# Accumulating the products of a 2x2 block scheme onto each other in PSUM, in a float32 hybrid-attention trunk

## The chip, the cores and the metric

One NeuronCore of a Trainium2 chip runs the whole program. The time is device microseconds of one execution; the median of three runs is given. Lower is better.

## The reference

Two layers of a post-norm trunk over a sequence of 512 positions with 1024 channels, in float32. Each layer projects its input once into ten parts and three gates, runs three mixers on them, and adds a SwiGLU feed-forward part with 2816 hidden channels:

```python
def reference(x, w_in, ...):
    for l in range(DEPTH):                               # DEPTH = 2, x is (1, 512, 1024)
        h = jnp.einsum('bsd,de->bse', x, w_in[l])
        rq, rk, rv, rg, cq, ck, cv, dq, dk, dv, gates = jnp.split(h, splits, axis=-1)
        o_a = _retention(rq, rk, rv, rg, ret_norm_g[l])   # 4 heads, dk 128, dv 256
        o_b = _chunk_attention(cq, ck, cv, ca_rel_bias[l])    # 8 heads of 64
        o_c = _diff_attention(dq, dk, dv, lam, ...)       # 4 heads, two maps each
        g = jax.nn.sigmoid(gates + b_merge[l]).reshape(B, S, N_BRANCHES, D)
        merged = sum over the three branches of g[:, :, i] * (o_i @ w_branch_i[l])
        mix = jnp.einsum('bsd,de->bse', merged, w_out[l])
        x = _layer_norm(DEEPNORM_ALPHA * x + mix, ln1_g[l], ln1_b[l])
        u = jnp.einsum('bsd,df->bsf', x, w_ffn_in[l])
        u_gate, u_up = jnp.split(u, 2, axis=-1)
        ...   # silu(u_gate) * u_up, w_ffn_out[l], second layer norm
```

## The kernel before

Every large operand is kept as a pair of float32r tiles, a high part and the rest, and each product of tiles is three matmuls: high by high, high by low weights, low by high (`mm3`, L122 to L124; which of the three carries which line depends on the side of the weights). A matmul has a 128x128 stationary and a 128x512 moving operand; one PSUM bank holds one 128x512 result, and there are 8 banks.

The wide projections that produce pairs of 512-column blocks (CV with DV, RV with RG, the feed-forward's input, the feed-forward's output) are computed as a 2x2 block problem with seven products instead of eight, in Winograd's form. The products are called m1, m2, y, x, v, g, h. Each has its own sum of activations, made once on VectorE (`Quarters.sums`, L290 ff., for the projections of x; `Twins.sums` for the feed-forward's hidden units), and its own weight block, which is a block of the weights or a sum of blocks (`Close` for the input projection, `Chain` for the feed-forward). Each product makes two 128-row halves, j = 0 and 1, and each half is 4 k-tiles x 3 = 12 matmuls in one PSUM bank where a block has 512 rows of contraction.

Weights go through three stages. SP loads a block of 128x2048 floats into one of four staging buffers; sums of blocks are made by an accumulating DMA that POOL issues (`Halves.more`, L178) or, in `Close`, by VectorE in place (L233, L239). Then ScalarE casts it to the high part (L259) and VectorE subtracts to get the low part (L260); high and low each have a pool of 3 buffers (`wsp`), which a product frees with its last matmul.

`u_two` (L732 ff.) runs one 2x2 problem. Before, m1, y, v and, where it comes ahead of x, g are copied out of PSUM by ScalarE (L746), and VectorE makes the seven sums of the scheme in SBUF for each half: three in `x` (L752 to L754), two in `last_right` (L761, L762), one each in `m2` (L770) and `h` (L775). The results go on to `left_done` and `right_done`, which split them into pairs or apply an activation. The feed-forward's output (`fout_items`) has the same scheme and adds its results to the residual with `plus` (L1302 to L1312), with two copies (L1332, L1339) and three sums (L1345 to L1347) in each half.

The order is a list of items written out by hand: an item is a weight specification and a function, followed by groups of small work (`s_q`, `s_dh`, `s_r1` and so on) which `between()` runs between halves. `run_items` fetches the weights of coming items until three are ready ahead. In each layer's mixer three such problems are named w (CV, DV), p and q (RV with RG, first and second half of the heads). A scheduler then orders the instructions of each engine; an engine runs them in that order, and waits where one is not ready. `w["c"]` and `w["a"]` in the list stand for loading the sums of weight blocks that g and y, h use, ahead of their items.

Of the kernel before, what the change touches and what calls it, by code (L numbers as in the profile page):

```python
# [17 lines left out]
P = 128  # L18
# [38 lines left out]
def trunk(ctx, tc, x_in, xT_in, w_in, ret_norm_g, da_norm_g, lq1, lk1, lq2, lk2, w_a, w_b, w_c, b_merge, w_out,  # L57
# [25 lines left out]
    def bank(name="ps"):  # L83
        return psp.tile([P, 512], F32, tag="ps", name=name)
# [33 lines left out]
        part_hi(pr.hi[:, cols], src, scale)  # L118
        part_lo(pr.lo[:, cols], src, pr.hi[:, cols], scale)

    def mm3(ps, lh, ll, rh, rl, start, stop):
        nc.tensor.matmul(ps, lh, rh, start=start, stop=False)  # L122
        nc.tensor.matmul(ps, lh, rl, start=False, stop=False)  # L123
        nc.tensor.matmul(ps, ll, rh, start=False, stop=stop)  # L124

    class Wt:

# [91 lines left out]
    class Close(Halves):  # L219
# [10 lines left out]
        def v(self):  # L230
            self.d = self.load(1, 1)
            b = self.block(self.d)
            nc.vector.tensor_add(self.d, self.d, self.a)  # L233
            return b

        def m2(self):
# [3 lines left out]
            return b  # L240

        def y(self):
            return self.block(self.__dict__.pop("a"))

        def x(self):
            return self.block(self.__dict__.pop("d"))
# [15 lines left out]
    class Quarters:  # L262
# [26 lines left out]
        def sums(self, t1, t2, scale=None):  # L289
            a, b = self.A, self.B  # L290
            sa, sb = g(name="sa"), g(name="sb")
            nc.vector.tensor_sub(sa[:, a], t1[:, b], t2[:, b])
            nc.vector.tensor_sub(sa[:, b], t1[:, a], sa[:, a])
            nc.vector.tensor_sub(sb[:, a], t2[:, a], sa[:, b])
            nc.vector.tensor_sub(sb[:, b], t1[:, b], t1[:, a])
            p12, p43 = Pair("s12"), Pair("s43")
            split(p12, sa, scale=scale)
            split(p43, sb, scale=scale)
            for name, pr, sl in (("y", p12, a), ("x", p12, b), ("v", p43, a), ("g", p43, b)):
                self.put(name, pr, sl)  # L300

    class Twins:
# [22 lines left out]
        def sums(self, a22):  # L325
            t = g(name="ta")
            nc.vector.tensor_sub(t, self.a21, a22)
            self.part("y", t)
            nc.vector.tensor_sub(t, self.a11, t)
            self.part("x", t)  # L330
            nc.vector.tensor_sub(self.a12, self.a12, t)
            self.part("v", self.a12)
            nc.vector.tensor_sub(self.a21, self.a21, self.a11)
            self.part("g", self.a21)
            self.part("h", a22)

    def product(acts, name, j, wt):

        ps, sl = bank("pf"), slice(P * j, P * j + P)
        for k in range(wt.nk):  # L340
            hi, lo = acts[k].use[name]
            mm3(ps, hi[:, sl], lo[:, sl], wt.hi[:, k], wt.lo[:, k], k == 0, k == wt.nk - 1)
        return ps

    def proj_T(act, wt, c0, nk=KT, ps=None, half=None):
# [261 lines left out]
    def layer(l):  # L607
# [123 lines left out]

        def u_two(hv, acts, left_done, right_done):  # L732

            t = {}

            def it(spec, name, use):
                def fn(wt):
                    for j in range(2):
                        use(j, product(acts, name, j, wt))
                        between()  # L740
                return [spec], fn

            def copy(to):
                def use(j, ps):
                    t[to, j] = g(name="t" + to)
                    nc.scalar.copy(t[to, j], ps)  # L746
                return use

            def x(j, ps):
                u, y, c = g(name="tu"), t["y", j], t.pop(("v", j))  # L750
                t["u", j] = u
                nc.vector.tensor_sub(u, ps, t.pop(("m1", j)))  # L752
                nc.vector.tensor_add(y, y, u)
                nc.vector.tensor_add(c, c, y)  # L754
                right_done(j, c)
                if ("g", j) in t:
                    last_right(j, t.pop(("g", j)))

            def last_right(j, c):
                y, u = t.pop(("y", j)), t["u", j]  # L760
                nc.vector.tensor_add(y, y, c)  # L761
                nc.vector.tensor_add(u, u, c)  # L762
                right_done(2 + j, y)

            def gg(j, ps):
                (last_right if ("u", j) in t else copy("g"))(j, ps)

            def m2(j, ps):
                c = g(name="tm")
                nc.vector.tensor_add(c, t["m1", j], ps)  # L770
                left_done(j, c)

            def h(j, ps):
                u = t.pop(("u", j))
                nc.vector.tensor_sub(u, ps, u)  # L775
                left_done(2 + j, u)

            use = {"x": x, "m2": m2, "g": gg, "h": h}
            return {"c": hv.ahead_c, "a": getattr(hv, "ahead_a", None),
                    **{k: it(getattr(hv, k), k, use.get(k) or copy(k)) for k in ("m1", "g", "v", "m2", "y", "x", "h")}}  # L780

        def rv_done(hp, t, c):
            rv[hp, t] = Pair("rv")
# [337 lines left out]

        w, p, q = u_two(Close(W, 0, 4, (CV, DV)), xq, v_away(cv, 64), v_away(dv, 128)), u_rvg(0), u_rvg(1)
        for (specs, fn), *groups in [
            (u_first(),), (u_gate(0, 1), [s_q(0)], [s_q(1), w["c"]]), (w["m1"], [], [s_q(2), w["a"]]), (u_gate(0, 2), [s_q(3)]),
            (w["g"],), (w["v"],), (w["m2"], [lam]), (w["y"], [p["c"]]), (w["x"],), (u_gate(0, 3),), (w["h"], [p["a"]]),
            (p["m1"], [s_dh(0)]), (p["g"], [], [s_r1(0)]), (p["v"], [s_dh(1)]), (p["m2"], [], [s_r1(1)]),
            (p["y"], [q["c"]]), (p["x"],), (u_rqk(rq, RQ, 1), [q["a"]]), (p["h"],),
            (q["m1"], [], [s_r2(0)]), (u_rqk(rk, RK, 1), [s_r2(1)], [s_r3(0)]), (q["g"], [], [s_r3(1)]),
            (q["v"], [s_dh(2)]), (q["m2"], [], [s_r1(2)]), (q["y"], [s_dh(3)]), (q["x"],), (u_cqk(0), [], [s_r1(3)]), (q["h"],),
            (u_gate(2, 0), [s_r2(2)], [s_r2(3), s_r3(2)]), (u_cqk(1), [s_r3(3)] + c(0)[0], c(0)[1]),  # L1130
            (u_branch(0, 0), c(1)[0] + [v_back(cv)], c(1)[1]), (u_branch(0, 1), *c(2)), (u_cqk(2), *c(3)),
            (u_branch(0, 2), *c(4)), (u_cqk(3), *c(5)), (u_branch(0, 3), *c(6)), (u_gate(2, 1), *c(7)),
            (u_dqk(0), *c(8)), (u_gate(1, 0), [v_back(dv)], [s_c3(7)] + d(0)[1]), (u_branch(1, 0), *d(1)), (u_dqk(1),),
            (u_gate(1, 1), *d(2)), (u_branch(1, 1), *d(3)), (u_dqk(2),),
            (u_gate(1, 2), *d(4)), (u_branch(1, 2), *d(5)), (u_dqk(3),),
            (u_gate(1, 3), *d(6)), (u_branch(1, 3), *d(7)), (u_gate(2, 2), [s_d4(2)], [s_d2(3)]),
            (u_gate(2, 3), [s_d3(3)], [s_d4(3)]),
            (u_branch(2, 0),), (u_branch(2, 1),), (u_branch(2, 2),), (u_branch(2, 3),),
        ]:
            item(specs, fn, *groups)  # L1140
# [175 lines left out]
        def fout_items(gi):  # L1316
# [2 lines left out]
            hv = Chain(w_ffn_out[l], r0, kh)  # L1319
            w = {}  # L1320

            def run(name, j, wt):
                return product([hid[r0 + k] for k in range(kh)], name, j, wt)

            def m1(wt):
                if gi == 0:
                    load_res(saved[2 * l])
                    x2["fresh"] = {(t, hf) for t in range(NT) for hf in range(2)}
                for j in range(2):
                    ps = run("m1", j, wt)  # L1330
                    w[j] = g(name="w")
                    nc.scalar.copy(w[j], ps)  # L1332
                    plus(j, 0, ps, ALU.add)

            def y(wt):
                for j in range(2):
                    ps = run("y", j, wt)
                    w["y", j] = g(name="wy")
                    nc.scalar.copy(w["y", j], ps)  # L1339

            def x(wt):
                for j in range(2):
                    ps = run("x", j, wt)
                    u = w.pop(j)
                    nc.vector.tensor_sub(u, ps, u)  # L1345
                    plus(2 + j, 0, u, ALU.subtract)
                    nc.vector.tensor_add(u, u, w.pop(("y", j)))  # L1347
                    plus(2 + j, 1, u, ALU.add)
                    plus(j, 1, u, ALU.add)

            def one(name, i, hf, op):
                def fn(wt):
                    for j in range(2):
                        plus(2 * i + j, hf, run(name, j, wt), op)
                return fn

            def gg(wt):
                for j in range(2):
                    ps = run("g", j, wt)
                    plus(2 + j, 1, ps, ALU.add)  # L1360
                    plus(2 + j, 0, ps, ALU.subtract)

            return {"c": hv.ahead_c, "m1": ([hv.m1], m1), "y": ([hv.y], y), "x": ([hv.x], x),
                    "m2": ([hv.m2], one("m2", 0, 0, ALU.add)), "v": ([hv.v], one("v", 0, 1, ALU.add)),
                    "g": ([hv.g], gg), "h": ([hv.h], one("h", 1, 0, ALU.add))}

        def fout_rest(hf):

# [108 lines left out]
```

## Time and profile before

| | |
|---|---|
| Median of 3 runs | 1894.03 us (1893.98 to 1894.27) |
| Span of the profiled execution | 1894.5 us, 0.5 us above that median |
| TensorE busy | 1881.4 us, 9170 matmuls |
| VectorE busy | 1355.1 us, 2159 instructions |
| ScalarE busy | 946.2 us, 1575 instructions |
| DMA | 285.11 MB, mean 150 GB/s |

Engines in the rows: PE is TensorE's matmuls, PEld its weight loads, DVE is VectorE, ACT ScalarE, POOL GpSimd, SP SyncE. A row of the groups view names the line, the engine, the operation, the tiles written and read, their count, the busy time in us, the mean ns of one, and behind the second bar the engine's idle time ahead of them with what ended it. A row of the timeline begins with the start and the duration in us; brackets hold the idle time before. A matmul's row lasts longer than the step to the next one, since matmuls overlap. Times are of one profiled execution.

### The profile page before, as it was taken

To read this page: it belongs to the slowest core of one execution; us is meant where nothing else is said; L and a number is where in the kernel's file an instruction comes from. 1 tells how busy PE (TensorE), PEld (TensorE's weight loads), DVE (VectorE), ACT (ScalarE), POOL (GpSimd) and SP (SyncE) were. 2 spreads that over 40 slices of the span, in tenths; PEclk is the share of its full clock that TensorE was granted. 3 is DMA by queue.
4 is the path that set the end of the run, shared out by engine and by line. 5 is a ranking of instruction groups with operands and counts; after the bars stand their busy time and mean duration, and the time that the engine had idled before them with its cause. 6 is when DMAs were issued, how large, how long until landed. Compare 5 with 4: busy or idle time off the path is not lost. (4 is left out here: it accounts for less than half of the span.)

```text
span 1894.5 us, 24166 instructions
## 1 busy us (share of the span) xinstructions
PE 1881.4 (99%) x9170; PEld 1584.9 (84%) x9170; DVE 1355.1 (72%) x2159; ACT 946.2 (50%) x1575; POOL 113.9 (6%) x141
## 2 busy tenths in 40 slices
PE   9999999999999999999999999999999999999998
PEld 7888888888888888888898888888888898888886
DVE  6788867577765866786687788666776668667866
ACT  5555555566634444543255546555765344344430
POOL 2000000000000000000010000000000000000000
PEclk9999999999999999999999999999999999999999
DMA  9585443332155686765475944533322637777561
GB/s 282 170 268 152 122 159 108 122 122 68 57 186 147 156 178 169 207 156 127 139 190 171 285 113 145 169 104 95 123 79 73 205 101 175 181 179 196 139 153 45
DMA packets 239348, 285.11 MB, mean 150 GB/s; under 512 B 8580, under 2 KB 147936, under 8 KB 239232
## 3 DMA queue, kind: packets, MB, share of 16 engines
q1 hardware_dynamic: 215232, 237.01, 38.1%
q0 software_dynamic: 24000, 46.56, 14.4%
q8 instruction: 72, 1.18, 0.3%
q14 instruction: 44, 0.36, 0.1%
HBM read 260.42 MB, written 23.12 MB: 150 GB/s over the span
## 5 line engine op out<-in xcount | busy, mean ns | idle before, releaser
L122 PE MATMUL pt<-xTh,wh 128*128 128x512 f32 (+1 forms) x1328 | 497.2, 375 | 2.3 <-ACT wh L154 2.0
L124 PE MATMUL pt<-xTh,wl 128*128 128x512 f32 (+1 forms) x1328 | 494.0, 372 | 0.0
L123 PE MATMUL pt<-xTl,wh 128*128 128x512 f32 (+1 forms) x1328 | 493.9, 372 | 0.0
L154 ACT CAST wh<-st 128x1024 fp32r<-128x1024 f32 (+1 forms) x236 | 220.2, 962 | 210.4 <-PE pt L123 91.1
L155 DVE TENSOR_TENSOR wl<-st,wh 128x1024 fp32r<-128x1024 f32 (+1 forms) x236 | 257.4, 1111 | 81.0 <-ACT wh L154 75.0
L260 DVE TENSOR_TENSOR wl<-st,wh 128x2048 fp32r<-128x2048 f32 x98 | 224.4, 2290 | 117.2 <-ACT wh L259 116.8
L122 PEld LDWEIGHTS pt<-xTh,wh 128*128 128x128 f32 x1328 | 250.1, 189 | 44.3 <-ACT wh L154 2.5
L124 PEld LDWEIGHTS pt<-xTh,wl 128*128 128x128 f32 x1328 | 250.5, 189 | 43.9
L123 PEld LDWEIGHTS pt<-xTl,wh 128*128 128x128 f32 x1328 | 250.9, 189 | 41.9
L259 ACT CAST wh<-st 128x2048 fp32r<-128x2048 f32 x98 | 187.5, 1913 | 157.4 <-PE pf L124 73.9
L124 PE MATMUL pf<-wh,xTl 128*128 128x512 f32 x240 | 93.4, 389 | 0.0
L123 PE MATMUL pf<-wl,xTh 128*128 128x512 f32 x240 | 93.4, 389 | 0.0
L122 PE MATMUL pf<-wh,xTh 128*128 128x512 f32 x240 | 93.4, 389 | 0.0
L122 PE MATMUL pf<-wh,s43h 128*128 128x512 f32 x192 | 75.5, 393 | 0.1
L122 PE MATMUL pf<-wh,s12h 128*128 128x512 f32 x192 | 74.9, 390 | 0.0
L123 PE MATMUL pf<-wl,s43h 128*128 128x512 f32 x192 | 74.8, 389 | 0.0
L124 PE MATMUL pf<-wh,s12l 128*128 128x512 f32 x192 | 74.7, 389 | 0.0
L123 PE MATMUL pf<-wl,s12h 128*128 128x512 f32 x192 | 74.7, 389 | 0.0
L124 PE MATMUL pf<-wh,s43l 128*128 128x512 f32 x192 | 74.2, 390 | 0.0
L382 ACT COPY sw<-pt 32x512 f32<-32x512 f32 (+1 forms) x96 | 55.7, 580 | 29.2 <-PE pt L124 28.0
L1207 DVE TENSOR_TENSOR fth<-fth,pt 128x512 f32<-128x512 f32 x28 | 19.2, 687 | 56.5 <-PE pt L124 56.2
L124 PEld LDWEIGHTS pf<-wh,xTl 128*128 128x128 f32 x240 | 45.1, 188 | 9.4
(362 smaller groups left out, 3570.7 us busy)
## 6 DMA issues: line engine op xcount, KB each, us to landing
st<-in_w_in SPq DMA_DIRECT2D x60, 1024.0 KB, 5.4
st<-in_w_ffn_in SPq DMA_DIRECT2D x56, 512.0 KB, 5.6
st<-in_w_ffn_out SPq DMA_DIRECT2D x20, 1024.0 KB, 5.0
st<-in_w_in SPq DMA_DIRECT2D x32, 512.0 KB, 5.0
st<-in_w_ffn_in SPq DMA_DIRECT2D x16, 1024.0 KB, 5.8
st<-in_w_ffn_in POOLq DMA_DIRECT2D x16, 1024.0 KB, 9.1
st<-in_w_ffn_out POOLq DMA_DIRECT2D x16, 1024.0 KB, 8.6
st<-in_w_in POOLq DMA_DIRECT2D x12, 1024.0 KB, 11.8
```

The lines of the kernel that those rows point to most:

```text
L122: nc.tensor.matmul(ps, lh, rh, start=start, stop=False)
L123: nc.tensor.matmul(ps, lh, rl, start=False, stop=False)
L124: nc.tensor.matmul(ps, ll, rh, start=False, stop=stop)
L154: return [nc.scalar.copy(self.hi[:, a:b], self.st[:, a:b]), nc.vector.tensor_sub(self.lo[:, a:b], self.st[:, a:b], f(self.hi[:, a:b]))]
L155: nc.vector.tensor_sub(self.lo[:, a:b], self.st[:, a:b], f(self.hi[:, a:b]))]
L259: nc.scalar.copy(self.hi, st)
L260: nc.vector.tensor_sub(self.lo, st, f(self.hi))
L382: nc.scalar.copy(sw[half * b:half * b + half], ps[half * o:half * o + half])
L1207: nc.vector.tensor_mul(t, t, pu)
```

## The change

Seven products are summed in the scheme in chains: m1 is part of x, g and h's results, y part of v's. After the change a product that builds on another writes into its PSUM bank without clearing it first, so the bank holds the running sum: x, g and h add onto m1's bank in this order, and v onto y's. Engines read the bank between the products. For this the activation sums of x, g and v take other signs (in `Quarters.sums` and in `Twins.sums`), so that additions in PSUM give what subtractions gave. In `u_two` three copies per half remain (m1, y, v, each into a result tile), and each of m2, x and g is one VectorE sum onto it; h is read straight from PSUM. In `fout_items` the seven products of a half go to the residual by seven `plus` calls; copies and sums in between are gone. In `Close`, the block "a" is used by y ahead of v. The order of products in the mixer is m1, y, v, m2, x, g, h instead of m1, g, v, m2, y, x, h, and the loads of "a" and "c" change places accordingly; the feed-forward's output keeps its order. `skip_group_check` is a flag for the program's builder.

```diff
-    def mm3(ps, lh, ll, rh, rl, start, stop):
+    def mm3(ps, lh, ll, rh, rl, start, stop, onto=False):
...
-        nc.tensor.matmul(ps, lh, rh, start=start, stop=False)
+        nc.tensor.matmul(ps, lh, rh, start=start, stop=False, skip_group_check=onto)
...
         def v(self):
             self.d = self.load(1, 1)
             b = self.block(self.d)
-            nc.vector.tensor_add(self.d, self.d, self.a)
+            nc.vector.tensor_add(self.d, self.d, self.__dict__.pop("a"))
             return b
...
         def y(self):
-            return self.block(self.__dict__.pop("a"))
+            return self.block(self.a)
...
             nc.vector.tensor_sub(sa[:, a], t1[:, b], t2[:, b])
-            nc.vector.tensor_sub(sa[:, b], t1[:, a], sa[:, a])
-            nc.vector.tensor_sub(sb[:, a], t2[:, a], sa[:, b])
-            nc.vector.tensor_sub(sb[:, b], t1[:, b], t1[:, a])
+            nc.vector.tensor_sub(sa[:, b], sa[:, a], t1[:, a])
+            nc.vector.tensor_add(sb[:, a], t2[:, a], sa[:, b])
+            nc.vector.tensor_sub(sb[:, b], t1[:, a], t1[:, b])
...
-    def product(acts, name, j, wt):
-        ps, sl = bank("pf"), slice(P * j, P * j + P)
+    def product(acts, name, j, wt, ps=None):
+        onto, sl = ps is not None, slice(P * j, P * j + P)
+        ps = ps if onto else bank("pf")
         for k in range(wt.nk):
             hi, lo = acts[k].use[name]
-            mm3(ps, hi[:, sl], lo[:, sl], wt.hi[:, k], wt.lo[:, k], k == 0, k == wt.nk - 1)
+            mm3(ps, hi[:, sl], lo[:, sl], wt.hi[:, k], wt.lo[:, k], k == 0 and not onto, k == wt.nk - 1, onto)
...
-            t = {}
+            t, onto = {}, {"x": "m1", "g": "m1", "h": "m1", "v": "y"}
-            def it(spec, name, use):
+            def it(name, use):
                 def fn(wt):
                     for j in range(2):
-                        use(j, product(acts, name, j, wt))
+                        t[name, j] = ps = product(acts, name, j, wt, t.pop((onto.get(name), j), None))
+                        if name in ("x", "g"):
+                            t["m1", j] = ps
+                        use(j, ps)
                         between()
...
+            def m2(j, ps):
+                c = t.pop(("c11", j))
+                nc.vector.tensor_add(c, c, ps)
+                left_done(j, c)
             def x(j, ps):
...
+                c = t.pop(("c12", j))
+                nc.vector.tensor_sub(c, c, ps)
                 right_done(j, c)
...
             def gg(j, ps):
-                (last_right if ("u", j) in t else copy("g"))(j, ps)
+                c = t.pop(("c22", j))
+                nc.vector.tensor_sub(c, c, ps)
+                right_done(2 + j, c)
...
             def h(j, ps):
-                u = t.pop(("u", j))
-                nc.vector.tensor_sub(u, ps, u)
-                left_done(2 + j, u)
+                left_done(2 + j, ps)
...
-            (q["m1"], [], [s_r2(0)]), (u_rqk(rk, RK, 1), [s_r2(1)], [s_r3(0)]), (q["g"], [], [s_r3(1)]),
-            (q["v"], [s_dh(2)]), (q["m2"], [], [s_r1(2)]), (q["y"], [s_dh(3)]), (q["x"],), (u_cqk(0), [], [s_r1(3)]), (q["h"],),
+            (q["m1"], [], [s_r2(0)]), (u_rqk(rk, RK, 1), [s_r2(1)], [s_r3(0)]), (q["y"], [], [s_r3(1)]),
+            (q["v"], [s_dh(2)]), (q["m2"], [], [s_r1(2)]), (q["x"], [s_dh(3)]), (u_cqk(0), [], [s_r1(3)]), (q["g"],), (q["h"],),
...
+            return {"c": hv.ahead_c, "m1": it("m1", (0, 0, add)), "y": it("y", (1, 1, add)), "x": it("x", (0, 1, sub)),
+                    "m2": it("m2", (0, 0, add)), "v": it("v", (0, 1, add)), "g": it("g", (1, 1, sub)), "h": it("h", (1, 0, add))}
```

More of the change, by code (lines that the diff above doesn't have):

```diff
@@ L119, in split @@
         part_lo(pr.lo[:, cols], src, pr.hi[:, cols], scale)
-    def mm3(ps, lh, ll, rh, rl, start, stop):
-        nc.tensor.matmul(ps, lh, rh, start=start, stop=False)
-        nc.tensor.matmul(ps, lh, rl, start=False, stop=False)
-        nc.tensor.matmul(ps, ll, rh, start=False, stop=stop)
+    def mm3(ps, lh, ll, rh, rl, start, stop, onto=False):
+        nc.tensor.matmul(ps, lh, rh, start=start, stop=False, skip_group_check=onto)
+        nc.tensor.matmul(ps, lh, rl, start=False, stop=False, skip_group_check=onto)
+        nc.tensor.matmul(ps, ll, rh, start=False, stop=stop, skip_group_check=onto)
     class Wt:
@@ L328, in sums @@
             self.part("y", t)
-            nc.vector.tensor_sub(t, self.a11, t)
+            nc.vector.tensor_sub(t, t, self.a11)
             self.part("x", t)
-            nc.vector.tensor_sub(self.a12, self.a12, t)
+            nc.vector.tensor_add(self.a12, self.a12, t)
             self.part("v", self.a12)
-            nc.vector.tensor_sub(self.a21, self.a21, self.a11)
+            nc.vector.tensor_sub(self.a21, self.a11, self.a21)
             self.part("g", self.a21)
             self.part("h", a22)
-    def product(acts, name, j, wt):
-        ps, sl = bank("pf"), slice(P * j, P * j + P)
+    def product(acts, name, j, wt, ps=None):
+        onto, sl = ps is not None, slice(P * j, P * j + P)
+        ps = ps if onto else bank("pf")
         for k in range(wt.nk):
             hi, lo = acts[k].use[name]
-            mm3(ps, hi[:, sl], lo[:, sl], wt.hi[:, k], wt.lo[:, k], k == 0, k == wt.nk - 1)
+            mm3(ps, hi[:, sl], lo[:, sl], wt.hi[:, k], wt.lo[:, k], k == 0 and not onto, k == wt.nk - 1, onto)
         return ps
@@ L732, in u_two @@
         def u_two(hv, acts, left_done, right_done):
-            t = {}
-            def it(spec, name, use):
+            t, onto = {}, {"x": "m1", "g": "m1", "h": "m1", "v": "y"}
+            def it(name, use):
                 def fn(wt):
                     for j in range(2):
-                        use(j, product(acts, name, j, wt))
+                        t[name, j] = ps = product(acts, name, j, wt, t.pop((onto.get(name), j), None))
+                        if name in ("x", "g"):
+                            t["m1", j] = ps
+                        use(j, ps)
                         between()
-                return [spec], fn
+                return [getattr(hv, name)], fn
             def copy(to):
@@ L747, in copy @@
                 return use
+            def m2(j, ps):
+                c = t.pop(("c11", j))
+                nc.vector.tensor_add(c, c, ps)
+                left_done(j, c)
             def x(j, ps):
[L750 to L754, printed above, removed]
-                right_done(j, c)
[L756 to L763, printed above, removed]
-            def gg(j, ps):
-                (last_right if ("u", j) in t else copy("g"))(j, ps)
[L768 to L771, printed above, removed]
-            def h(j, ps):
-                u = t.pop(("u", j))
-                nc.vector.tensor_sub(u, ps, u)
-                left_done(2 + j, u)
-            use = {"x": x, "m2": m2, "g": gg, "h": h}
-            return {"c": hv.ahead_c, "a": getattr(hv, "ahead_a", None),
-                    **{k: it(getattr(hv, k), k, use.get(k) or copy(k)) for k in ("m1", "g", "v", "m2", "y", "x", "h")}}
+                c = t.pop(("c12", j))
+                nc.vector.tensor_sub(c, c, ps)
+                right_done(j, c)
+            def gg(j, ps):
+                c = t.pop(("c22", j))
+                nc.vector.tensor_sub(c, c, ps)
+                right_done(2 + j, c)
+            def h(j, ps):
+                left_done(2 + j, ps)
+            use = {"m1": copy("c11"), "m2": m2, "y": copy("c22"), "v": copy("c12"), "x": x, "g": gg, "h": h}
+            return {"c": hv.ahead_c, "a": getattr(hv, "ahead_a", None), **{k: it(k, fn) for k, fn in use.items()}}
         def rv_done(hp, t, c):
@@ L1123, in layer @@
         for (specs, fn), *groups in [
[L1124 to L1127, printed above, removed]
-            (q["m1"], [], [s_r2(0)]), (u_rqk(rk, RK, 1), [s_r2(1)], [s_r3(0)]), (q["g"], [], [s_r3(1)]),
-            (q["v"], [s_dh(2)]), (q["m2"], [], [s_r1(2)]), (q["y"], [s_dh(3)]), (q["x"],), (u_cqk(0), [], [s_r1(3)]), (q["h"],),
+            (u_first(),), (u_gate(0, 1), [s_q(0)], [s_q(1), w["a"]]), (w["m1"], [], [s_q(2)]), (u_gate(0, 2), [s_q(3), w["c"]]),
+            (w["y"],), (w["v"],), (w["m2"], [lam]), (w["x"], [p["a"]]), (u_gate(0, 3),), (w["g"],), (w["h"], [p["c"]]),
+            (p["m1"], [s_dh(0)]), (p["y"], [], [s_r1(0)]), (p["v"], [s_dh(1)]), (p["m2"], [], [s_r1(1)]),
+            (p["x"], [q["a"]]), (u_rqk(rq, RQ, 1),), (p["g"], [q["c"]]), (p["h"],),
+            (q["m1"], [], [s_r2(0)]), (u_rqk(rk, RK, 1), [s_r2(1)], [s_r3(0)]), (q["y"], [], [s_r3(1)]),
+            (q["v"], [s_dh(2)]), (q["m2"], [], [s_r1(2)]), (q["x"], [s_dh(3)]), (u_cqk(0), [], [s_r1(3)]), (q["g"],), (q["h"],),
             (u_gate(2, 0), [s_r2(2)], [s_r2(3), s_r3(2)]), (u_cqk(1), [s_r3(3)] + c(0)[0], c(0)[1]),
@@ L1320, in fout_items @@
             w = {}
[L1322 to L1349, printed above, removed]
@@ L1351, in one, with it @@
-            def one(name, i, hf, op):
+            def it(name, *adds):
                 def fn(wt):
+                    if name == "m1" and gi == 0:
+                        load_res(saved[2 * l])
+                        x2["fresh"] = {(t, hf) for t in range(NT) for hf in range(2)}
+                    on = {"x": "m1", "g": "m1", "h": "m1", "v": "y"}.get(name, name)
                     for j in range(2):
-                        plus(2 * i + j, hf, run(name, j, wt), op)
-                return fn
@@ L1357, in gg @@
[L1357 to L1365, printed above, removed]
+                        w[on, j] = product([hid[r0 + k] for k in range(kh)], name, j, wt, w.pop((on, j), None))
@@ new lines, in fn @@
+                        for i, hf, op in adds:
+                            plus(2 * i + j, hf, w[on, j], op)
+                        if name in ("m2", "v", "h"):
+                            w.pop((on, j))
+                return [getattr(hv, name)], fn
+            add, sub = ALU.add, ALU.subtract
+            return {"c": hv.ahead_c, "m1": it("m1", (0, 0, add)), "y": it("y", (1, 1, add)), "x": it("x", (0, 1, sub)),
+                    "m2": it("m2", (0, 0, add)), "v": it("v", (0, 1, add)), "g": it("g", (1, 1, sub)), "h": it("h", (1, 0, add))}
```

## The prediction

> **What bounds the kernel now.** The first page of the profile gives the span and the share of each engine.
>
> ```profile
> span 1894.5 us, 24166 instructions
> PE 1881.4 (99%) x9170; PEld 1584.9 (84%) x9170; DVE 1355.1 (72%) x2159; ACT 946.2 (50%) x1575; POOL 113.9 (6%) x141
> ```
>
> TensorE (PE) has work in 1881.4 of 1894.5 us, so 13.1 us are all that could be won without fewer or faster matmuls. Read second: the view of waits, for TensorE alone, in full, and the last row of TensorE in the timeline.
>
> ```profile
> PE pt L122 <- ACT wh L154: 2.0, 1, 2.0
> PE warm L578 <- POOL ident masks.py:199: 1.5, 1, 1.5
> PE px L504 <- DVE z L495: 0.6, 2, 0.3
> PE pt L122 <- ACT xTh L596: 0.2, 1, 0.2
> ```
>
> ```profile
> 1885.44 0.39 PE L124 MATMUL pf<-wh,hidl 128*128 128x512 f32 x1
> ```
>
> The last matmul ends at 1885.83; the 8.67 us behind it are the last layer norm and the store. The waits on L154, on the identity and on L596 (3.7 us together) stand at the start, before the first projection has its weights. Neither stretch is touched by the change: the last product is h before and after, with one vector operation behind it. 13.1 - 8.67 - 3.7 leaves 0.7 us in the whole body, about the 0.6 of L504. So no relief of VectorE (DVE), ScalarE (ACT) or the DMA queues can bring more than 0.7 us. Everything else that the change can do is to make TensorE wait where it doesn't now.
>
> Third, the windows view of a stretch of the FFN, where the 2x2 products are the main work.
>
> ```profile
> 700.00:800.00 100.00, 100.00 (x452) 82.19 (x451) 70.14 (x77) 48.08 (x58) 7.72 (x6) 1.00 0.71 174
> ```
>
> Columns: TensorE, its weight loads, VectorE, ScalarE and POOL busy, granted clock, DMA share, GB/s. TensorE is busy in all 100 us at full clock, VectorE in 70.
>
> **The sums that go.** The groups view prices them (first and last kinds of each, us in total, mean ns of one).
>
> ```profile
> L752 DVE TENSOR_TENSOR tu<-pf,tm 128x512 f32<-128x512 f32 x20 | 13.7, 683 | 0.0
> L761 DVE TENSOR_TENSOR ty<-ty,tg 128x512 f32<-128x512 f32 x12 | 8.2, 684 | 0.0
> L1347 DVE TENSOR_TENSOR w<-w,wy 128x512 f32<-128x512 f32 x8 | 5.3, 685 | 0.0
> L746 ACT COPY tg<-pf 128x512 f32<-128x512 f32 x12 | 6.6, 591 | 10.7 <-PE pf L124 10.7
> L1332 ACT COPY w<-pf 128x512 f32<-128x512 f32 x8 | 4.2, 581 | 0.0
> ```
>
> Two layers with three input groups (w, p, q) and FFN-in's chains make 20 halves of u_two, as x20 shows; FFN-out has 8. In u_two 7 sums become 3: 80 fewer. In FFN-out 3 sums and 8 accumulations into the residual become 7 accumulations: 32 fewer. 112 x 0.684 = 76.6 us of VectorE. Of copies the 12 of g and 16 in FFN-out go: 28 x 0.59 = 16.5 us of ScalarE. By the first part they are worth between 0 and 0.7 us; I take 0, because the waits that they could shorten (L504) are in the layer norm, not among the products. The matmuls stay at 9170, the DMA instructions at their number. The negated sums of activations (Quarters, Twins) replace instructions one for one: nothing.
>
> **The waits that come.** x, g and h now write m1's bank, and v writes y's. Each product must wait until the read of the one below it is over. Where other products stand between, 12 to 24 matmuls and more cover a 0.6-us read. The shortest cover is g to h: h's first half follows g's second half, 12 matmuls after g's first half has ended. Matmuls of this shape follow each other at 0.227 us (in the rows below, 22 steps from 190.35 to 195.34), so the cover is 2.72 us for a subtraction of 0.68. It fails only with a long instruction ahead of it in VectorE's queue: a rival, below. Taken: 0.
>
> **The order that moves.** The groups w, p and q now run m1, y, v, m2, x, g, h instead of m1, g, v, m2, y, x, h. Weight loads move with it: the sums behind "a" are loaded one or more items earlier, those behind "c" later; loads and their accumulations are still issued by SP and POOL at a fetch that runs three weight blocks ahead, 3 x 24 x 0.227 = 16 us, and the page has them land sooner (its last figure, from issue to landing):
>
> ```profile
> st<-in_w_in SPq DMA_DIRECT2D x60, 1024.0 KB, 5.4
> ...
> st<-in_w_in POOLq DMA_DIRECT2D x12, 1024.0 KB, 11.8
> ```
>
> So I take 0; an accumulation issued one product late would still have 5 us. One spot costs. In the compiled order of the changed kernel, after the second rk projection of group q, TensorE has: 8 transposes (L861, now L853), the 24 matmuls of y, 8 transposes, and then x's first two matmuls, which need its high weights, then its third, with the low weights; only seven x matmuls later come m2 and v. Before, the same place held 8 transposes, 24 matmuls of g, 8 transposes and v, whose weights had long been cast. The weight pool has 3 buffers; y, v and m2 hold them. x is the fourth, so its cast (L259) can't start until y's last matmul has ended, and its subtraction (L260) follows the cast. The instructions on ScalarE and VectorE stand there in the same order before and after; only the weights that are cast differ. So the trace of before shows when they can be ready. Timelines of TensorE, ScalarE and VectorE:
>
> ```profile
> 189.01 0.39 PE L124 MATMUL pt<-xTh,wl 128*128 128x512 f32 x1
> 189.24 0.93 PE L861 MATMUL prt<-ident,ro 128*128 128x128 f32 x7
> ...
> 190.35 0.40 PE L123 MATMUL pf<-wl,s43h 128*128 128x512 f32 x1
> ...
> 195.34 0.39 PE L124 MATMUL pf<-wh,s43l 128*128 128x512 f32 x1
> 195.58 1.03 PE L861 MATMUL prt<-ident,ro 128*128 128x128 f32 x8
> 196.37 0.48 PE L122 MATMUL pf<-wh,s43h 128*128 128x512 f32 x1
> 196.68 0.40 PE L123 MATMUL pf<-wl,s43h 128*128 128x512 f32 x1
> 196.91 0.39 PE L124 MATMUL pf<-wh,s43l 128*128 128x512 f32 x1
> ```
>
> ```profile
> 195.78 1.91 ACT L259 CAST wh<-st 128x2048 fp32r<-128x2048 f32 x1 [3.46 <-PE pf L124]
> 199.26 1.07 ACT L746 COPY tg<-pf 128x512 f32<-128x512 f32 x2
> ```
>
> ```profile
> 194.56 2.29 DVE L239 TENSOR_TENSOR st<-st 128x2048 f32<-128x2048 f32 x1
> 196.76 0.68 DVE L386 TENSOR_TENSOR rot<-rot,sw 128x512 f32<-128x512 f32 x1
> 197.71 2.29 DVE L260 TENSOR_TENSOR wl<-st,wh 128x2048 fp32r<-128x2048 f32 x1 [0.27 <-ACT wh L259]
> 199.92 0.68 DVE L112 TENSOR_TENSOR rqkl<-rot,rqkh 128x512 fp32r<-128x512 f32 x1
> 200.53 2.06 DVE L114 SCALAR_TENSOR_TENSOR oal<-prt,colv,oah 128x512 fp32r<-128x512 f32 x3
> ```
>
> The 24th matmul issues at 195.34 and ends at 195.73; the cast starts at 195.78 and ends at 197.69; the subtraction starts at 197.71 and ends at 200.00. TensorE wants x's first matmul at 196.37, so it waits 1.32 us. It issues two, and wants the third at 196.91 + 1.32 = 198.23, but the low weights are there at 200.00: 1.77 more. Together 200.00 - 196.91 = 3.1 us, and some hundredths to hand on. Behind it seven matmuls of x end their issue at 201.6: m2's bank must have been read by the first of the three L114, which ends at 200.53 + 0.69 = 201.2, and v's bank by the two copies, here tg, that end at 200.3. Both are in time, by 0.4 and more, so nothing is added. The second layer has the same spot:
>
> ```profile
> 1138.02 0.39 PE L124 MATMUL pf<-wh,s43l 128*128 128x512 f32 x1
> ```
>
> ```profile
> 1138.82 2.29 DVE L260 TENSOR_TENSOR wl<-st,wh 128x2048 fp32r<-128x2048 f32 x1 [0.27 <-ACT wh L259]
> ```
>
> 1138.82 + 2.29 - 1138.02 = 3.1. TensorE has nothing else queued that it could take, since its instructions run in order, and no slack later, so both stalls reach the end: 2 x 3.1 and the handing on, +6.3 us. Other spots of the new order (v after y in the first group, FFN-in's second chain) I estimate by the same kind of sum at +-0.3 each, with both signs, net 0, and give them +-1.5 in the range. The profiled span is 1894.5, the median of the runs 1894.0; the difference of 6.3 is put on the median: **1900.3 us**.
>
> **Rivals.** *The clock falls with the stall.* At the start of the trace one wait of 2.03 us is followed by slow matmuls (timeline of TensorE; then the windows view, whose third value from the right is the granted clock):
>
> ```profile
> 7.77 0.80 PE L122 MATMUL pt<-xTh,wh 128*128 128x512 f32 x1 [2.03 <-ACT wh L154]
> 8.36 0.63 PE L123 MATMUL pt<-xTl,wh 128*128 128x512 f32 x1
> 8.79 0.63 PE L124 MATMUL pt<-xTh,wl 128*128 128x512 f32 x1
> ```
>
> ```profile
> 9.00:10.00 1.00, 1.00 (x3) 0.78 (x3) 1.00 (x3) 0.84 (x2) 0.54 (x1) 0.50 1.11 302
> 11.00:12.00 1.00, 1.00 (x6) 0.82 (x5) 0.74 (x2) 0.01 (x1) 0.00 (x0) 0.98 1.17 269
> ```
>
> Steps of 0.43 us for about 3.3 us, 8 matmuls at 0.20 extra: 1.6 us for each stall, 3.2 for both, 1903.5. For it: the wait here is of that size, 1.3 and 1.8 with two matmuls between. Against: those two matmuls break it, and the start had other idle time ahead of it. Chance 0.17. The Trainium skill, "TensorE: Matmul & The Clock Gate", section "Part 1: The HAM clock gate", says that half clock returns only after a whole idle window of about 3.4 us, counted in windows that run free of the kernel; by that rule neither wait is enough and the time stays at the forecast. The trace does not bear it out cleanly: a wait of 2.03 us stood before the half clock.
>
> *Every h waits for its g.* If a 2.29-us subtraction starts just ahead of g's read, the read ends 2.97 us after g, plus 0.16 by which a matmul's 0.39 outlasts its 0.23 step, against a cover of 2.72: 0.4 late. In 28 places at most 11.5 us, 1911.8. It decides once VectorE is more than 1.9 us behind as g's half ends. For it: fetches put a cast and a subtraction at about every product. Against: the VectorE queue loses sums exactly there, and a subtraction starts at the end of a product two or three items back, not at g's half. Chance 0.09; a part of it, some 3 us, is likelier than all. The Trainium skill, "PSUM — Partial Sum Buffer", section "The four PSUM rules", allows a synchronised read in the middle of an accumulation, so that the read is a wait and not an error; no row of before shows such a read.
>
> *Not slower: x's weights are ready.* It decides if x's subtraction ends 3.1 us earlier, by 196.91, or its cast finds a buffer that y doesn't hold, or if only one layer has the spot (+3.1). Then the time is 1894 less at most 0.7: 1893.3 to 1897.2. For it: in the trace of before no weight of a 2x2 product was waited for. Against: the cast in the trace starts 0.05 after the matmul that frees the buffer, with no wait left to take out. Chance 0.09. Faster by over 0.2% would need more than the 0.7 us that exist, so a fault in my reading of the page: 0.03.
>
> **How the numbers follow.** Forecast 0.62, clock 0.17, h 0.09, not slower 0.09, faster 0.03. 0.2% is 3.8 us, about what a measurement of this kernel can tell from no change. The range: at the low end 1896.0, between both cases; at the high end 1905.0, which takes in the clock with 1.5 of unknown. It leaves out the full price of h and the time under 1896. Slower is 0.62 + 0.17 + 0.09 = 0.88, same 0.09, faster 0.03.
>
> **What the profile after would show.** Right: TensorE's waits list L122 and L123 (x's products, in pf) behind ACT wh L259 with about 1.3 and DVE wl L260 with about 1.8, twice each, near 196.4 and 1137.5; TENSOR_TENSOR 112 fewer on VectorE, about 1279 us busy; TensorE's matmuls still 9170 and the end of its last one about 6 us later. Clock rival: a granted clock under 1.00 right behind these places. h rival: waits of pf on DVE lines of the subtractions in gg and plus, 28 times. Wrong: none of these waits, or a TensorE wait in a third place that is larger.

## The result and the profile after

The changed kernel takes 1904.7 us (median of 4 runs, 1903.87 to 1905.45) against 1894.15 before: ratio 1.0053, 95% interval 1.0038 to 1.0067. A second measurement gave 1903.59 against 1894.12, ratio 1.0046 (1.0034 to 1.0059). So it is 9.5 to 10.5 us slower; 6.3 were forecast. Executions of every kernel here, the one before too, fall into two groups some 1.8 us apart, by the traces according to whether the slow matmuls at the start last until 5 to 7 us or until about 11, so a median of four can lie between the groups; both profiles compared here are of the longer one.

The first page of the profile after, its span and engines:

```profile
span 1903.7 us, 24003 instructions
PE 1886.1 (99%) x9170; PEld 1588.1 (83%) x9170; DVE 1290.6 (68%) x2047; ACT 931.2 (49%) x1547; POOL 114.0 (6%) x141
```

VectorE has 112 instructions and 64.5 us less, ScalarE 28 and 15.0 less, and the span is 9.2 us longer. (A run's time is about 1.8 us above its span, here 1905.45 and 1903.7, so the span of before, 1894.5, is to be set beside spans and not beside the median.) The view of waits of the changed kernel, TensorE alone, in full:

```profile
PE pf L123 <- DVE wl L260: 3.2, 2, 1.6
PE pf L122 <- ACT wh L259: 2.2, 2, 1.1
PE warm L579 <- POOL ident masks.py:199: 1.5, 1, 1.5
PE pt L122 <- ACT wh L154: 0.8, 1, 0.8
PE px L505 <- DVE z L496: 0.6, 2, 0.3
PE pf L122 <- ACT rph L106: 0.4, 2, 0.2
```

The first two rows are new: x's products wait for the low weights twice and for the high weights twice, 5.4 us as this view counts idle time (it counts from the end of a matmul's row, which outlasts the step to the next one). The last row is new too. The timelines of TensorE, ScalarE and VectorE at the first of the two places, in the first layer:

```profile
195.37 0.39 PE L124 MATMUL pf<-wh,s12l 128*128 128x512 f32 x1
195.60 1.03 PE L853 MATMUL prt<-ident,ro 128*128 128x128 f32 x8
197.75 0.73 PE L122 MATMUL pf<-wh,s12h 128*128 128x512 f32 x2 [1.11 <-ACT wh L259]
200.08 0.50 PE L123 MATMUL pf<-wl,s12h 128*128 128x512 f32 x1 [1.59 <-DVE wl L260]
200.42 0.39 PE L124 MATMUL pf<-wh,s12l 128*128 128x512 f32 x1
...
203.39 0.39 PE L124 MATMUL pf<-wh,s43l 128*128 128x512 f32 x1
```

```profile
195.80 1.90 ACT L259 CAST wh<-st 128x2048 fp32r<-128x2048 f32 x1 [3.46 <-PE pf L124]
```

```profile
197.73 2.29 DVE L260 TENSOR_TENSOR wl<-st,wh 128x2048 fp32r<-128x2048 f32 x1 [0.26 <-ACT wh L259]
```

y's last matmul issues at 195.37; the cast into its buffer runs from 195.80 to 197.70, the subtraction from 197.73 to 200.02. x's first two matmuls issue at 197.75, the third at 200.08. Without the wait the first would stand at 196.39 and the third at 196.93: 3.15 us. The second layer has the same places, and something more:

```profile
1142.29 0.73 PE L122 MATMUL pf<-wh,s12h 128*128 128x512 f32 x2 [1.12 <-ACT wh L259]
1144.62 0.80 PE L123 MATMUL pf<-wl,s12h 128*128 128x512 f32 x1 [1.59 <-DVE wl L260]
1145.21 0.63 PE L124 MATMUL pf<-wh,s12l 128*128 128x512 f32 x1
...
1150.74 0.40 PE L124 MATMUL pf<-wh,s43l 128*128 128x512 f32 x1
```

```profile
1143.00:1144.00 1.00, 0.03 (x1) 0.00 (x0) 1.00 (x1) 1.00 (x3) 0.00 (x0) 0.94 0.00 0
...
1146.00:1150.00 4.00, 4.00 (x11) 3.06 (x10) 1.80 (x3) 0.05 (x1) 0.00 (x0) 0.50 0.96 326
```

The matmuls behind the stall take 0.63 instead of 0.39 and follow at 0.43 instead of 0.227, and the windows view gives the granted clock, third from the right, as 0.50. The 0.94 of the window ahead means that the clock fell at 1143.88, inside the second idle piece and not behind it. The last slow step ends at 1150.74. The fourteen steps from 1144.62 to there take 6.12 us; the same fourteen in the first layer, from 200.08 to 203.39, take 3.31. That is 2.8 us more. So in this execution: two stalls 6.3, half clock behind one of them 2.8, two waits of h (below) 0.8. That is 9.9; the last matmul of the kernel issues 9.14 us later than before (1885.44 to 1894.58). The rest is 0.5 less in the first 15 us and small differences in other places, of both signs.

```profile
1894.58 0.39 PE L124 MATMUL pf<-wh,hidl 128*128 128x512 f32 x1
```

### The profile page after: what moved, and what is told of

It reads as the page before. It is cut to its first block, busy times and chain, and to the rows that moved or that the text cites. A ratio compares the mean times of both kernels' runs of the same rounds, so it can differ in the third digit from the quotient of the medians.

```text
span 1903.7 us, 24003 instructions
## 1 busy us (share of the span) xinstructions
PE 1886.1 (99%) x9170; PEld 1588.1 (83%) x9170; DVE 1290.6 (68%) x2047; ACT 931.2 (49%) x1547; POOL 114.0 (6%) x141
## 5 line engine op out<-in xcount | busy, mean ns | idle before, releaser
L750 ACT COPY tc<-pf 128x512 f32<-128x512 f32 x60 | 34.1, 586 | 54.2 <-PE pf L124 53.0
```

## The experiments

Theory S: x in group q is taken ahead of its weights, 3.1 us in each layer, and the stall lets the clock fall, for the rest. Rival A: the accumulation is dear in itself. Rival B: the new order of products is, whatever is accumulated.

**The same kernel again** (no edit).

> The changed kernel once more, unedited, for a second trace. Theory S (the two stalls for x's weights in group q cost 2 x 3.1 us, and half clock behind them the rest): both stalls at the same places and of the same length, 1.3 and 1.8 us each; matmuls at a step of 0.43 us behind one or both of them, in blocks of about 3.3 us, and the time between 1903.8 and 1905.5 according to how many blocks there are, 1.6 us for each. Rival A (the accumulation itself is dear, by waits for reads spread over the 28 places): no relation between the time and the slow blocks.

It took 1903.59 us (1902.44 to 1904.60 in 5 runs), 0.2 under the range that was expected. In its trace the two rows of the waits for x's weights are those of the first trace, figure for figure. The timeline of TensorE and two windows:

```profile
197.72 0.52 PE L123 MATMUL pf<-wl,s12h 128*128 128x512 f32 x1 [1.59 <-DVE wl L260]
...
198.47 0.63 PE L122 MATMUL pf<-wh,s12h 128*128 128x512 f32 x1
```

```profile
198.00:199.00 1.00, 1.00 (x4) 0.76 (x4) 1.00 (x3) 1.00 (x2) 0.00 (x0) 0.53 0.14 10
...
1143.00:1144.00 1.00, 0.18 (x1) 0.19 (x2) 1.00 (x2) 1.00 (x4) 0.00 (x0) 0.77 0.00 0
```

The stalls are the same. The slow steps now stand behind both: eight in the first layer, 1.6 us, and seven in the second, 1.45 us, where the first trace had none behind the first stall and fourteen behind the second, 2.8 us. By the windows, the clock fell at 198.06 and at 1143.55 (0.53 and 0.77 are mixtures of 1.00 and 0.50), each time for 3.41 us. So the part of the clock varies in place between executions and was about the same in sum in these two, 3.0 and 2.8; that it explains each run's time can't be shown from two traces.

**Something between y and v.** Two items of the list change places in q:

```diff
-            (q["m1"], [], [s_r2(0)]), (u_rqk(rk, RK, 1), [s_r2(1)], [s_r3(0)]), (q["y"], [], [s_r3(1)]),
+            (q["m1"], [], [s_r2(0)]), (q["y"], [s_r2(1)], [s_r3(0)]), (u_rqk(rk, RK, 1), [], [s_r3(1)]),
```

> In group q the second rk projection comes behind y instead of ahead of it, so its 24 matmuls lie between y and v, x's weights have time, and nothing waits for the cast that needs y's buffer; accumulation, sums and all else as in the changed kernel. Theory S: both stalls and the slow blocks behind them go, 10 to 11 us less than the changed kernel, 1893.5 to 1894.8, as before. Rival A: the accumulation is unchanged, so 1903 or more.

1893.90 us; ratio to before 0.9998 (0.9989 to 1.0007). The view of waits of TensorE in full:

```profile
PE warm L579 <- POOL ident masks.py:199: 1.5, 1, 1.5
PE pt L122 <- ACT wh L154: 0.7, 1, 0.7
PE px L505 <- DVE z L496: 0.6, 2, 0.3
PE pf L122 <- ACT rph L106: 0.4, 2, 0.2
PE pt L122 <- ACT xTh L597: 0.3, 1, 0.3
```

Neither wait for x's weights is there, no slow matmul stands in the body, and the time is that of before. All the accumulation is still in, so Rival A falls: the whole loss that can be told hangs on that one place of the order.

**The order alone.** The kernel before with the list of items of the changed one and, in Close, y ahead of v:

```diff
-            (q["m1"], [], [s_r2(0)]), (u_rqk(rk, RK, 1), [s_r2(1)], [s_r3(0)]), (q["g"], [], [s_r3(1)]),
-            (q["v"], [s_dh(2)]), (q["m2"], [], [s_r1(2)]), (q["y"], [s_dh(3)]), (q["x"],), (u_cqk(0), [], [s_r1(3)]), (q["h"],),
+            (q["m1"], [], [s_r2(0)]), (u_rqk(rk, RK, 1), [s_r2(1)], [s_r3(0)]), (q["y"], [], [s_r3(1)]),
+            (q["v"], [s_dh(2)]), (q["m2"], [], [s_r1(2)]), (q["x"], [s_dh(3)]), (u_cqk(0), [], [s_r1(3)]), (q["g"],), (q["h"],),
...
-            nc.vector.tensor_add(self.d, self.d, self.a)
+            nc.vector.tensor_add(self.d, self.d, self.__dict__.pop("a"))
...
-            return self.block(self.__dict__.pop("a"))
+            return self.block(self.a)
```

> The kernel before with the new order of products alone (m1, y, v, m2, x, g, h, with the loads of a and c moved), sums and copies as before, each product in a bank of its own. Theory S: x needs a free bank like the others, so it isn't taken ahead of v, whose weights are there; no stall, 1893.5 to 1895.0. Rival B (the order alone makes the stall, by the moved weight loads and sums): two stalls of about 3 us, 1900 or more.

1893.64 us, ratio 0.9996 (0.9987 to 1.0005). Waits of TensorE, in full:

```profile
PE warm L578 <- POOL ident masks.py:199: 1.5, 1, 1.5
PE pt L122 <- ACT wh L154: 0.6, 1, 0.6
PE px L504 <- DVE z L495: 0.6, 2, 0.3
```

No stall, so Rival B falls too. (The copies are not quite as before: with g behind x its 12 copies go, 1563 ScalarE instructions against 1575.) It takes both: in the new order v follows y, and with the accumulation v waits until ScalarE has read y's bank, while x, which adds onto a bank long read, waits for no bank. That this is why the scheduler puts x there is read from the compiled orders of the two kernels; it was not tried by itself.

**Work in the stall.** Ahead of x in q, zeros are added onto m1's bank, and x is queued behind them:

```diff
+    def fill(ps, acts):
+        with tc.issue_after(end_mm["y"].ins):
+            for i in range(14):
+                end_mm["fill"] = nc.tensor.matmul(ps[0:64], zero, acts[0].wide, start=False, stop=False, skip_group_check=True)
```

> The changed kernel with 14 matmuls of a zero stationary operand (128x64, moving 128x512) added onto m1's bank ahead of x in group q, so 3.2 us of work that adds zero stands in each stall. Theory S, with the clock as the second part: the weights are late as before, so the 6.3 us stay, but TensorE is never idle for long, so the slow steps go: 1900.3 to 1901.5, 3 to 4 us under the changed kernel. If the clock is not the second part, the time stays at 1904 to 1905.

1900.96 us: 2.6 to 3.7 under the two medians of the changed kernel, inside the expected range. Waits of TensorE, in full:

```profile
PE warm L589 <- POOL ident masks.py:199: 1.5, 1, 1.5
PE px L515 <- DVE z L506: 0.6, 2, 0.3
PE pf L123 <- ACT rph L107: 0.4, 2, 0.2
PE pt L123 <- ACT wh L155: 0.3, 1, 0.3
```

TensorE does 28 useless matmuls (6.4 us) in place of two stalls, and no step of 0.43 us stands in the body. The zeros end just ahead of the weights: in the first layer the subtraction for the low weights ends at 197.94, and the first matmul that needs them issues at 198.00. So this is the price of late weights by itself, 6.8 us over before (6.3 at the stalls and h's wait, told last), and the rest of the loss is the clock's.

**Half the fill.** As above with `range(7)`.

> As fill, with 7 zero matmuls instead of 14: 1.6 us of each stall are filled, and one idle piece of some 1.5 us is left instead of two of 1.1 and 1.6. The 6.3 us of late weights stay. If the clock falls after any idle piece of that length, 1902.5 to 1904; if it takes more idle time than that, as with 14: 1900.5 to 1901.5. Theory S is open on this; it only says that the time is one of these two.

1901.03 us, as with 14, though the zeros take only half the time: it is the weights that set it. One wait is left in each layer, and no slow step behind it:

```profile
PE pf L124 <- DVE wl L261: 2.8, 2, 1.4
```

**Weights in two halves.**

```diff
-            nc.scalar.copy(self.hi, st)
-            nc.vector.tensor_sub(self.lo, st, f(self.hi))
+            for a in range(0, nk, nk // parts):
+                b = a + nk // parts
+                nc.scalar.copy(self.hi[:, a:b], st[:, a:b])
+                nc.vector.tensor_sub(self.lo[:, a:b], st[:, a:b], f(self.hi[:, a:b]))
...
         def x(self):
-            return self.block(self.__dict__.pop("d"))
+            return Staged(self.__dict__.pop("d"), self.kh, 2)
```

> The changed kernel with x's weights in the input projection cast and subtracted in two halves (k-tiles 0 and 1, then 2 and 3), for x's first matmuls need the first half alone. Theory S, from rows of the kernels so far: the first half of the cast takes 0.96 us and is ready at 196.8, 0.4 after TensorE wants it; VectorE is busy until 197.4 with what stands ahead, the first half of the subtraction takes 1.15 and ends at 198.6, 1.4 more. So stalls of 1.8 us in each layer instead of 3.1, 3.6 in all: 1897.9 to 1898.8 where the clock holds, up to 1901 where it falls behind both. If the stall hung on y's buffer alone and not on the length of cast and subtraction, it would stay at 3.1 and the time at 1903 or more.

1898.84 us, ratio 1.0024 (1.0014 to 1.0034). From the waits and the timeline of TensorE:

```profile
PE pf L123 <- DVE wl L262: 2.0, 2, 1.0
...
PE pf L122 <- ACT rph L106: 1.4, 2, 0.7
```

```profile
196.57 0.73 PE L122 MATMUL pf<-wh,s12h 128*128 128x512 f32 x2 [0.26 <-ACT wh L261]
198.32 0.50 PE L123 MATMUL pf<-wl,s12h 128*128 128x512 f32 x1 [1.02 <-DVE wl L262]
```

The first stall shrinks from 1.11 to 0.26 as the view counts, the second from 1.59 to 1.02, so the length of the cast and of the subtraction sets them, as Theory S has it; the clock holds. But the row with rph grew to 1.4: h's wait, told last, takes 0.7 in each layer instead of 0.2; TensorE reaches that place 1.72 us earlier than in the changed kernel (g's last matmul at 234.31 against 236.03), and g's subtraction ends only 1.22 earlier (235.27 against 236.49). The time is 0.04 us over the expected range for a clock that holds, and that wait is something the expectation had left out.

**FFN-out as before.** On the version with rk behind y, fout_items and Twins are put back. The hidden units of the second group still take their sums from Quarters with the new signs, so in this kernel some products enter with signs that don't fit, and its output is not the reference's; the work is the same.

> The version with the second rk projection behind y, with FFN-out and its sums of hidden units as in the kernel before (8 halves with 11 VectorE operations and two copies instead of 7 and none); only the input projection and FFN-in accumulate in PSUM. By the forecast's bound, 32 VectorE operations more are hidden behind TensorE: within 0.7 us of the version with it, 1893.3 to 1894.7. If the accumulation in FFN-out itself gains or loses time at the waits for reads, the two differ by more.

1894.48 us against 1893.90, both medians of 11 runs, in different sets of runs; ratio to the kernel before in its own set 0.9999 (0.9991 to 1.0008). The medians are 0.6 apart and the intervals overlap: 32 VectorE operations and 16 copies more cost no time that can be told.

**Room between g and h.** On the version with rk behind y:

```diff
-            ... (q["x"], [s_dh(3)]), (u_cqk(0), [], [s_r1(3)]), (q["g"],), (q["h"],),
+            ... (q["x"], [s_dh(3)]), (q["g"], [], [s_r1(3)]), (u_cqk(0),), (q["h"],),
```

What it is about stands in the timelines of VectorE, ScalarE, TensorE and its weight loads of the version without it:

```profile
229.83 0.76 DVE L806 TENSOR_TENSOR rtmp<-psr,dh 128x384 f32<-128x384 f32 x2
230.50 0.68 DVE L765 TENSOR_TENSOR tc<-tc,pf 128x512 f32<-128x512 f32 x1
```

```profile
230.67 0.62 ACT L106 CAST rph<-rtmp 128x512 fp32r<-128x512 f32 x1 [2.03 <-DVE rtmp L806]
```

```profile
230.76 0.39 PE L124 MATMUL pf<-wh,s43l 128*128 128x512 f32 x1
231.32 0.47 PE L122 MATMUL pf<-wh,xTh 128*128 128x512 f32 x1 [0.18 <-ACT rph L106]
```

```profile
231.29 0.19 PEld L122 LDWEIGHTS pf<-wh,xTh 128*128 128x128 f32 x1 [0.57 <-ACT rph L106]
```

h's first matmul writes the bank that L765 reads until 231.18. The view names ScalarE's cast, which ends at 231.29, just as the weight load for h starts. In x's stalls a load starts 0.05 to 0.06 us after what releases it (the cast ends at 197.70 and the load starts at 197.75; the subtraction ends at 200.02 and the load starts at 200.08), so the cast ends too late to be what h waits for. That leaves the subtraction for g as the likeliest.

> The version with the second rk projection behind y, and in group q the first chunk-attention projection (with s_r1(3) ahead of it) between g and h instead of between x and g. The trace of the version without this shows TensorE 0.34 us late at h's first matmul in each layer (231.32 and 1172.5), where VectorE's subtraction for g stands behind two products with the decay and ends at 231.18. Theory: with 24 matmuls and more between g and h that wait goes in both layers, 0.7 us less: 1893.2, at the edge of what can be told; the trace decides. If the wait hangs on ScalarE's cast, as the trace names it, it stays.

1893.07 us, ratio to before 0.9994 (0.9985 to 1.0003). Waits of TensorE, in full:

```profile
PE warm L579 <- POOL ident masks.py:199: 1.5, 1, 1.5
PE px L505 <- DVE z L496: 0.6, 2, 0.3
PE pt L122 <- ACT wh L154: 0.4, 1, 0.4
```

The wait is gone in both layers, and the median is 0.8 lower than without this edit, which ran in another set, and 1.1 lower than before in the same set of runs. The 24 matmuls would cover a wait for the cast as well, so the run doesn't tell the two apart; what does is that lag of 0.05 us. That it beats the kernel before is not shown, as its interval includes 1; that it is not slower by more than 0.03% is.

## Why the prediction was right or wrong

**What bounds it: right.** 64.5 us less of VectorE and 15.0 less of ScalarE brought nothing that can be told: the version with all the accumulation and no stall is at 1893.90 against 1894.12. Their size was a little too high (76.6 and 16.5), since the term multiplied each row's duration, and consecutive instructions overlap: behind a row of 0.68 the next one starts after 0.60.

**The order that moves: right, to 0.1 us.** x's cast was put at 195.78 and started at 195.80, the subtraction at 197.71 to 200.00 and ran from 197.73 to 200.02, and each stall was given 3.1 us and took 3.1. Nothing was late behind it, as forecast. The experiment that takes it away gave back the whole loss. One reserve in this part was summed wrongly: an accumulation issued one product late doesn't have 5 us left, since 16.3 less 5.4 is 10.9 and the row of these DMAs says 11.8 from issue to landing. No wait of TensorE hung on it, so the term of 0 held all the same.

**The clock: the step that failed.** The forecast held the clock at full speed and gave the other case 0.17, at 1903.5; that is where the kernel is. The price of that rival (8 steps at 0.20, 1.6 us for each stall, 3.2 for both) was close in sum, 2.8 and 3.0 in the two traces; its place was not right: once fourteen steps behind one stall, once eight and seven. The argument against it, that the two matmuls between the waits break the idle time, was wrong: with 1.1 and 1.6 us idle around two matmuls the clock fell in three of four stalls seen. It held with one idle piece of 1.4 us, with 0.3 and 1.0, and with none.

The traces say more. A block of half clock lasted 3.413 us in the second trace and 6.826, twice that, in the first. The two falls of the second trace lie 945.49 us apart, 277 times 3.4133; in the first, the rise at 10.66, at the start, and the fall at 1143.88 lie 332 times that apart. So in these traces the clock changed only on a grid of 3.41 us, whose place differed from one execution to the next. In the 3.41 us up to each fall TensorE was idle, by the ends of its rows, for 2.0 us in the first trace, for 2.35 and 2.45 in the second, and for 2.1 in the trace of before, at its start. Counted back on that grid from 1143.88, the stall in the first layer of the first trace lay across two stretches with 1.1 and 1.6 us idle, and there the clock held. This fits a clock that falls by the idle time summed within one stretch of the grid, with the limit somewhere between 1.6 and 2.0 us of 3.41; the two matmuls in between did not reset it. No run moved the grid on purpose, so the rule is read from these traces alone. The versions with 7 zeros and with half weights have 1.4 and 1.3 us idle in all, under that limit wherever the grid lies.

The Trainium skill, "TensorE: Matmul & The Clock Gate", section "Part 1: The HAM clock gate", asks for an idle window of about 3.4 us, in windows that run free of the kernel. The length of the blocks and the grid agree with such windows. That the window must be idle throughout does not agree: 2.0 to 2.45 us of 3.41 were enough.

**h behind g: a term that was set to 0.** The rival was given 28 places at 0.4 us or a part of them. The traces of the changed kernel show 2, in group q, 0.38 us each, where two products with the decay stand ahead of g's subtraction in VectorE's queue, and not a 2.29-us subtraction as the rival had it. The other 26 places show no wait. So of the measured loss over the forecast, some 0.8 is this and 2.8 to 3.0 the clock, less 0.3 to 0.4 of small differences in other places.

The sign was right, and the range held the median, by 0.3 us, because its upper end had been set to take the clock in; two of the four runs, at 1905.4, lie above it. The likeliest case itself was 3.3 to 4.4 us short.

## What to carry to other kernels

Where TensorE is busy all the time, as here, work taken from other engines can be worth nothing, and what counts is what the edit does to the order: look in the compiled order for a matmul that comes ahead of the buffer its weights are cast into. An accumulation in PSUM frees the product from needing a bank and binds it to a reader, so a scheduler may take products in another order than the list has them. A stall of 3 us on TensorE should be priced with the matmuls at half clock behind it, here up to half as much again, and filling it with useless matmuls shows the two parts apart. Two matmuls in the middle of such a stall didn't always keep the clock, since the idle time around them adds up; seven more at its start did.

## What the runs showed that was not expected

The clock fell to 0.50 within or just behind three of four stalls that had 2.7 us of idle time broken by two matmuls, for 3.41 us twice and for 6.83 us once. By the traces, whether it fell went by how the stall lay on a grid of 3.41 us. It didn't fall with 1.4 us idle in one piece. Seven matmuls of zeros in the stall were enough to keep it at full speed: 1901.03 us with 7, 1900.96 with 14, 1903.6 to 1904.7 without.
